# Four gate/up slabs side by side in the first FFN, and scores by pairs of heads on alternating row halves, in a two-layer encoder trunk

## The chip, the cores and the metric

The kernel runs on one core of a Trainium2 chip. The core has a matrix engine (TensorE, PE in the rows; its weight loads are PEld), VectorE (DVE), ScalarE (ACT), GpSimd (POOL) and SyncE (SP), which here issues nearly all the weight loads. The metric is the device time of one execution in microseconds, as the median of several runs.

## The reference, cut to what matters

Two layers, each with three sub-layers on 256 tokens of width 1024: a SwiGLU FFN of width 2816, a mixer with two attention branches, and a second FFN. Each is preceded by an RMS norm that is modulated with a scale and a shift taken from the conditioning `c`, and is added with a gate taken from it too.

```python
mod = c_act @ ada_w[l] + ada_b[l]
sh1, sc1, g1, sh2, sc2, g2, sh3, sc3, g3 = jnp.split(mod, N_ADA, axis=-1)
n1 = modulate(rms_norm(h, norm_g[l, 0]), sh1, sc1)
h = h + 0.5 * g1[:, None, :] * swiglu(n1, ffn_wg[l, 0], ffn_wu[l, 0], ffn_wd[l, 0])
...
# diff_attention, the second branch: two softmax maps m, four heads h, head width 64
sc = jnp.einsum('bqmhd,bsmhd->bmhqs', qi, k) * scale
p = jax.nn.softmax(sc + bias[None, None], axis=-1)      # bias = -slope * |q - k|
w = (p[:, 0] - lam * p[:, 1])
```

Inputs, weights and output are float32.

## The kernel before, in words

**Precision.** Every weight half (128 x 1024) is split into a part `whi`, rounded to the matrix engine's format, and the remainder `wlo`: ScalarE casts `whi` (line 302), VectorE subtracts (line 303). Activations are split likewise into `nh` and `nl`. A product is then three matmuls, hi-hi, lo-hi, hi-lo (`mm3`, lines 85 to 87).

**Loads.** `stream` is a list, written out by hand, of units of 128 x 2048 float32 (1 MB) in the order in which they are used. `load_next` issues the next one on SP's queue into a ring of four buffers `raw` (the first twenty units as two DMAs of half a unit). `pump(n)` takes the next n halves of the stream: a weight half is split into two of 23 slots, a `col` half becomes a column sum with `cb` on VectorE (line 235), from which the modulation's scale `ma` and shift `msh` come, and a `gate` half is added up to the residual's gate. A buffer's release lets SP issue the next load. `queue` orders such an instruction behind the one noted in `behind` for its engine.

**The order of the work.** The program's order on each engine follows from the order in which the code emits it, shifted where the planner of the tile framework sees an operand that is not ready. The code lists it by hand, in the mixer above all.

**The beginning (lines 1183 to 1203 and `first`, line 1133).** The two token halves are squared (half 0 on ScalarE, half 1 on VectorE), GpSimd makes `rstd`, VectorE scales (`xs`, line 360), TensorE transposes and ScalarE copies to `xsT`. A slab is 256 gate and 256 up columns, with the contraction of 1024 in eight chunks k; a column step `C` makes the scale and shift of two chunks, and `mod_k` turns these into `nh` and `nl`. The string `START` (line 39) has the order: `C` a pair of column units, `a` the unit with the first four chunks of the next slab, `b` the one with its last four. `go` multiplies a slab with two chunks as soon as both are there (24 matmuls). The first four slabs are done so, in four pairs of banks; then follow the down products of the finished slabs and the other seven slabs.

**The second branch's scores (`b_scores`, line 855).** For each of four heads, and each token half t: a matmul of 512 columns puts the distance bias into a bank (`idn`, a scaled identity, times `dist`), and for both maps m three matmuls of 64 rows add q.k. The heads' 64 rows are the lower or the upper half of the array by hd % 2. Then VectorE takes the maxima and ScalarE the exponentials. `b_norm` combines the two maps, `b_T` transposes them, `b_out` multiplies with v. The mixer's list (lines 1006 to 1047) puts these between the gate products `gate_mm(j, half)`, 24 matmuls each. The first branch's `a_scores` (line 788) takes two heads that lie in different row halves in turn, into two banks. All these banks are of one kind, `gen`, of which there are four.

Of the kernel before, what the change touches and what calls it, by code (L numbers as in the profile page):

```python
# [13 lines left out]
F32 = mybir.dt.float32  # L14
F32R = mybir.dt.float32r
# [4 lines left out]
P = 128  # L20
# [18 lines left out]
START = "CaCaCaabCbbb"  # L39


def trunk(tc, a):
    nc = tc.nc
    with (
# [158 lines left out]
        def load_next():  # L203
            if nload[0] < len(stream):
                u = stream[nload[0]]
                nload[0] += 1
                raw = wp.tile([P, 2048], F32, tag="raw", bufs=RAW_BUFS, name=nm("raw"))
                src = SRC[u[0]](u)
# [82 lines left out]
        def pump(n=1):  # L291
            while n > 0 and pos[0] < len(stream):
# [6 lines left out]
                if isw:  # L299
# [4 lines left out]
                    halves[u + (i,)] = (hi, lo)  # L304
# [25 lines left out]
        class Norm:  # L330
# [11 lines left out]
            def square_dve(self, hf):  # L342
                junk = b2("sq")
                x = h[self.t][:, hf * 512:(hf + 1) * 512]
                nc.vector.tensor_tensor_reduce(junk, x, x, 1.0 / 1024.0, 0.0, op0=ALU.mult, op1=ALU.add,
                                               accum_out=self.ssq[:, hf:hf + 1])
# [9 lines left out]
            def scale(self):  # L356
                self.xs = []
                for hf in range(2):
                    xs = b2("xs")
                    self.dve = nc.vector.tensor_scalar(xs, h[self.t][:, hf * 512:(hf + 1) * 512], self.rstd[:, 0:1], None,  # L360
# [166 lines left out]
        def ffn(i, nT, norm1, first, nT_next):  # L527
# [25 lines left out]
            if first is not None:  # L553
                first(hT, down)
                start = START.count("a")
                for idx in range(start == 4, start - 1):
                    down(idx)
# [115 lines left out]
        def mixer(i, nT, norm1, consts, nT_next):  # L673
# [177 lines left out]

            xs = {}
            wTs = {}

            def b_scores(hd):
                slope = 2.0 ** (-8.0 * (hd + 1) / 4.0)
                pr = slice((hd % 2) * 64, (hd % 2 + 1) * 64)
                idn = sb.tile([P, P], F32R, tag="idn", bufs=2, name=nm("idn"))
                nc.scalar.mul(idn, ident, -8.0 * slope)
                for t in range(2):  # L860
                    tok = slice(t * P, (t + 1) * P)
# [430 lines left out]
```

## Time and profile before

| | us |
|---|---|
| median of 3 runs (lowest, highest) | 1130.22 (1130.12, 1131.29) |
| the profiled execution | 1128.88 |
| its span, first to last instruction | 1127.1 |
| TensorE busy in it | 1104.9 |
| VectorE busy | 867.4 |
| ScalarE busy | 588.4 |

Busy times of the engines overlap. A busy TensorE is not one at its peak: matmuls are pipelined, so a row's duration (0.28 us for 256 columns) is longer than the distance from one start to the next, and the distance is what counts for the sum. The page has the chip's HBM read at 239 GB/s over the whole span.

### The profile page before, as it was taken

Reading aid. Unit: us, or ns where it says so; the run is one execution under the profiler, and the core shown is the slowest. Engines: PE = TensorE matmul, PEld = TensorE weight load, DVE = VectorE, ACT = ScalarE, POOL = GpSimd, SP = SyncE. Lnnn points to the kernel's source line nnn. Section 1 sums busy time; section 2 is a strip of 40 time slices with the busy share of each in tenths; the row PEclk is TensorE's granted clock in tenths of the full one; section 3 lists DMA queues with packets and bytes.
Section 4 is the critical chain, followed back from the end, with each engine's and each line's share of the span. In section 5 each row is a group of like instructions: output and inputs, shape, how many; then the busy total and the mean of one; then the engine's idle time right before and its main releaser. Section 6 shows DMA issues by size and latency. Waiting matters only on the chain.

```text
span 1127.1 us, 19136 instructions
## 1 busy us (share of the span) xinstructions
PE 1104.9 (98%) x7774; PEld 1019.7 (90%) x7774; DVE 867.4 (77%) x1334; ACT 588.4 (52%) x911; POOL 43.8 (4%) x52
## 2 busy tenths in 40 slices
PE   5999999999999999999999999999999999999997
PEld 3999999898899899999989999989889998999996
DVE  6996985899877798896489886469986778865543
ACT  4553474558664563435355544435766447544432
POOL 1000000130000000000000000004000100000000
PEclk9999999999999999999999999999999999999999
DMA  9997985368645389988439977543755454876500
GB/s 336 370 376 284 377 337 185 113 252 321 217 184 185 113 321 355 355 334 315 150 130 352 368 289 274 193 158 144 276 216 182 146 197 151 311 269 224 196 27 38
DMA packets 42584, 271.11 MB, mean 241 GB/s; under 512 B 5624, under 2 KB 6392, under 8 KB 12544
## 3 DMA queue, kind: packets, MB, share of 16 engines
q1 hardware_dynamic: 40036, 267.93, 64.2%
q10 hardware_dynamic: 2460, 1.96, 0.6%
q8 instruction: 61, 1.00, 0.3%
q14 instruction: 27, 0.22, 0.1%
HBM read 268.82 MB, written 1.05 MB: 239 GB/s over the span
## 4 chain that ended last, share of the span: by engine, by line
PE 91%; DVE 6%; issue 1%; DMA 1%; ACT 1%; POOL 1%; POOLq 0%; DVEq 0%
PE dn L87 7%; PE dn L86 7%; PE dn L85 7%; PE g L87 7%; PE u L85 7%; PE g L85 7%; PE u L87 7%; PE g L86 7%; PE u L86 7%; PE gt L85 3%; PE gt L86 3%; PE gt L87 3%; DVE wlo L303 1%; PE yb L87 1%; PE yb L86 1%; PE yb L85 1%
## 5 line engine op out<-in xcount | busy, mean ns | idle before, releaser
L303 DVE TENSOR_TENSOR wlo<-raw,whi 128x1024 fp32r<-128x1024 f32 x364 | 437.9, 1222 | 145.8 <-PE u L86 88.5
L302 ACT CAST whi<-raw 128x1024 fp32r<-128x1024 f32 x364 | 374.3, 1051 | 223.4 <-PE u L87 83.7
L85 PE MATMUL g<-nh,whi 128*128 128x256 f32 x656 | 185.0, 282 | 3.7 <-ACT nh L1145 3.7
L87 PE MATMUL g<-nl,whi 128*128 128x256 f32 x656 | 184.8, 282 | 1.6 <-DVE nl L1148 1.6
L85 PE MATMUL u<-nh,whi 128*128 128x256 f32 x656 | 184.6, 281 | 0.0
L86 PE MATMUL u<-nh,wlo 128*128 128x256 f32 x656 | 184.6, 281 | 0.0
L86 PE MATMUL g<-nh,wlo 128*128 128x256 f32 x656 | 184.4, 281 | 0.0
L87 PE MATMUL u<-nl,whi 128*128 128x256 f32 x656 | 184.3, 281 | 0.0
L85 PE MATMUL dn<-whi,hh 128*128 128x512 f32 (+1 forms) x358 | 138.5, 387 | 0.0
L87 PE MATMUL dn<-wlo,hh 128*128 128x512 f32 (+1 forms) x358 | 138.2, 386 | 0.0
L86 PE MATMUL dn<-whi,hl 128*128 128x512 f32 (+1 forms) x358 | 138.2, 386 | 0.0
L85 PEld LDWEIGHTS g<-nh,whi 128*128 128x128 f32 x656 | 123.8, 189 | 5.5 <-ACT nh L1145 4.1
L87 PEld LDWEIGHTS g<-nl,whi 128*128 128x128 f32 x656 | 125.7, 192 | 1.9 <-DVE nl L1148 1.9
L87 PEld LDWEIGHTS u<-nl,whi 128*128 128x128 f32 x656 | 126.0, 192 | 0.1
L86 PEld LDWEIGHTS g<-nh,wlo 128*128 128x128 f32 x656 | 124.2, 189 | 1.3
L86 PEld LDWEIGHTS u<-nh,wlo 128*128 128x128 f32 x656 | 124.1, 189 | 0.0
L85 PEld LDWEIGHTS u<-nh,whi 128*128 128x128 f32 x656 | 123.9, 189 | 0.0
L235 DVE CUSTOM_DVE_ANT_0 raw<-raw,cb 128x1024 f32<-128x1024 f32 x96 | 114.8, 1220 | 8.9 <-DMA raw<-in_ada_t_dram 8.9
L87 PEld LDWEIGHTS dn<-wlo,hh 128*128 128x128 f32 x358 | 67.3, 188 | 13.6
L85 PEld LDWEIGHTS dn<-whi,hh 128*128 128x128 f32 x358 | 67.3, 188 | 12.3
L86 PEld LDWEIGHTS dn<-whi,hl 128*128 128x128 f32 x358 | 67.3, 188 | 12.2
L508 ACT ACTIVATE sg<-g 128x512 f32<-128x512 f32 x41 | 24.5, 598 | 97.7 <-PE g L87 97.5
(202 smaller groups left out, 1888.5 us busy)
## 6 DMA issues: line engine op xcount, KB each, us to landing
raw<-in_w_gu_dram SPq DMA_DIRECT2D x79, 1024.0 KB, 5.9
raw<-in_w_d_dram SPq DMA_DIRECT2D x41, 1024.0 KB, 5.9
raw<-in_ada_t_dram SPq DMA_DIRECT2D x40, 1024.0 KB, 5.4
raw<-in_ada_g_dram SPq DMA_DIRECT2D x24, 1024.0 KB, 6.4
raw<-in_w_in_dram SPq DMA_DIRECT2D x16, 1024.0 KB, 4.8
raw<-in_w_gate_dram SPq DMA_DIRECT2D x16, 1024.0 KB, 4.9
raw<-in_w_gu_dram SPq DMA_DIRECT2D x18, 512.0 KB, 6.0
raw<-in_ada_t_dram SPq DMA_DIRECT2D x16, 512.0 KB, 6.1
```

The source lines that it names most:

```text
L85: nc.tensor.matmul(out, Lh, Rh, start=start, stop=False, skip_group_check=True)
L86: nc.tensor.matmul(out, Ll, Rh, start=False, stop=False, skip_group_check=True)
L87: nc.tensor.matmul(out, Lh, Rl, start=False, stop=stop, skip_group_check=True)
L235: queue("dve", nc.vector.tensor_tensor_reduce(r, r, cb, 1.0, 0.0, op0=ALU.mult, op1=ALU.add, accum_out=col[:, k:k + 1]))
L302: queue("act", nc.scalar.copy(hi, r))
L303: queue("dve", nc.vector.tensor_tensor(lo, r, hi.bitcast(F32), op=ALU.subtract))
L508: nc.scalar.activation(sg, g, AF.Silu)
```

## The change

The string `START` goes; `SIDE = 4` takes its place. At the beginning the stream is now four times: two column units, then two `side` units, each of which holds the same two K chunks of two slabs. `go` runs a step's 24 matmuls as eight hi-hi, eight lo-hi and eight hi-lo, and every step covers all four slabs. In `mod_k` the remainder `nl` is noted in `behind`, as is the second square of token half 1; the scaling `xs` at the beginning moves to ScalarE.

In the mixer `b_scores(hd)` becomes `b_scores(pair, t)`: two bias matmuls into two banks, then the twelve products of 64 rows, one head's and the other's in turn. The four `idn` are made once and kept. `b_norm` follows the pairs, and the hand-written list is rearranged.

```diff
-START = "CaCaCaabCbbb"
+SIDE = 4
@@ the stream
-                g = {x: [("gu", 0, 0, i, k) for i in range(START.count(x))] for k, x in enumerate("ab")}
-                w = [u for u in w if u not in g["a"] + g["b"]]
-                for x in START:
-                    if x == "C":
-                        stream += [c.pop(0), c.pop(0)]
-                    else:
-                        stream.append(g[x].pop(0))
+                w = [u for u in w if not (u[0] == "gu" and u[3] < SIDE)]
+                for j in range(4):
+                    stream += [c.pop(0), c.pop(0)]
+                    stream += [("side", j, p) for p in range(SIDE // 2)]
@@ load_next
+                if u[0] == "side":
+                    _, j, pr = u
+                    for i in range(2):
+                        x = slice((j % 2) * 1024, (j % 2 + 1) * 1024)
+                        nc.sync.dma_start(raw[:, i * 1024:(i + 1) * 1024], a["w_gu"][0, 0, 2 * pr + i, j // 2][:, x])
@@ Norm
-                nc.vector.tensor_tensor_reduce(junk, x, x, 1.0 / 1024.0, 0.0, op0=ALU.mult, op1=ALU.add,
+                self.dve = nc.vector.tensor_tensor_reduce(junk, x, x, 1.0 / 1024.0, 0.0, op0=ALU.mult, op1=ALU.add,
...
+                    if on_act:
+                        nc.scalar.activation(xs, h[self.t][:, hf * 512:(hf + 1) * 512], AF.Identity, scale=self.rstd[:, 0:1])
@@ the second branch
+            idns = mc.setdefault("idn", [])
+            for hd in range(len(idns), 4):
+                idns.append(const(f"idn{hd}", [P, P], F32R))
+                nc.scalar.mul(idns[hd], ident, -8.0 * 2.0 ** (-8.0 * (hd + 1) / 4.0))
...
+            def b_scores(pair, t):
+                tok = slice(t * P, (t + 1) * P)
+                scs = []
+                for hd in (2 * pair, 2 * pair + 1):
                     sc = gen("scb")
-                    nc.tensor.matmul(sc.rearrange("p (m k) -> p m k", m=2), idn, dist[:, t:t + 1, :].broadcast_to([P, 2, S]),
+                    nc.tensor.matmul(sc.rearrange("p (m k) -> p m k", m=2), idns[hd], dist[:, t:t + 1, :].broadcast_to([P, 2, S]),
                                      start=True, stop=False, skip_group_check=True)
-                    for m in range(2):
-                        ch = m * 2 + hd // 2
-                        score_mm(sc[:, m * 256:(m + 1) * 256], (st["qdT"], (pr, ch, tok)), (st["kdT"], (pr, ch, slice(0, S))), False)
+                    scs.append(sc)
+                for m in range(2):
+                    ch = m * 2 + pair
+                    for x, y in ((0, 0), (1, 0), (0, 1)):
+                        for e in range(2):
+                            pr = slice(e * 64, (e + 1) * 64)
+                            nc.tensor.matmul(scs[e][:, m * 256:(m + 1) * 256], st["qdT"][x][pr, ch, tok], st["kdT"][y][pr, ch, :],
+                                             start=False, stop=y == 1, skip_group_check=True)
@@ the mixer's list
-            b_scores(0)
+            b_scores(0, 0)
             gate_mm(1, 0)
             a_T(1, 0)
             gate_mm(1, 1)
             a_T(1, 1)
-            b_norm(0)
-            b_scores(1)
+            b_norm(0, 0)
+            b_scores(0, 1)
             gate_mm(2, 0)
             a_pv(1)
+            gate_mm(2, 1)
+            b_norm(0, 1)
+            b_scores(1, 0)
+            gate_mm(3, 0)
             b_T(0)
-            gate_mm(2, 1)
-            b_norm(1)
-            b_scores(2)
-            gate_mm(3, 0)
             gate_mm(3, 1)
             b_T(1)
-            b_norm(2)
-            b_scores(3)
+            b_norm(1, 0)
+            b_scores(1, 1)
             free(4)
             cap_w[0] = CAP2
             gate_mm(4, 0)
             gate_mm(4, 1)
+            b_norm(1, 1)
+            gate_mm(5, 0)
             b_T(2)
-            b_norm(3)
-            gate_mm(5, 0)
+            gate_mm(5, 1)
             b_T(3)
-            gate_mm(5, 1)
             b_out(0)
@@ first
             def mod_k(u):
                 pump(4)
+                pump(1)
...
-                nc.vector.tensor_tensor(nl[:, kk, :], nf, nh[:, kk, :].bitcast(F32), op=ALU.subtract)
+                behind["dve"] = nc.vector.tensor_tensor(nl[:, kk, :], nf, nh[:, kk, :].bitcast(F32), op=ALU.subtract)
...
+                for x, y in ((0, 0), (1, 0), (0, 1)):
+                    W, N = (wh, wl)[x], (nh, nl)[y]
+                    for k in (2 * u, 2 * u + 1):
+                        for c in range(2):
+                            for j, bank in ((0, g), (1, ub)):
...
+            for u in range(4):
+                mod_k(u)
+                if u % 2 == 1:
+                    free(1)
+                for sl in range(SIDE):
+                    go(sl, u)
+                    pump(1)
+                    if u == 3:
+                        if sl == 3:
+                            down(0)
+                        hT[sl] = gate_up_act(*banks[sl])
+                        pump(1)
@@ the beginning
                 if t == 1:
                     n.square_dve(hf)
+                    behind["dve"] = n.dve
...
-            n.scale()
+            n.scale(True)
```

## Rows read from the trace of the kernel before

**Rows 1.** The page: engines' busy us and share; casts' busy us, mean ns, idle before.
```profile
PE 1104.9 (98%) x7774; PEld 1019.7 (90%) x7774; DVE 867.4 (77%) x1334; ACT 588.4 (52%) x911; POOL 43.8 (4%) x52
...
L302 ACT CAST whi<-raw 128x1024 fp32r<-128x1024 f32 x364 | 374.3, 1051 | 223.4 <-PE u L87 83.7
```
**Rows 2.** TensorE's waits, 28 to 1110 us: us in total, times, longest.
```profile
PE nt L369 <- DVE xs L360: 1.0, 1, 1.0
PE pt L831 <- ACT p L820: 0.2, 1, 0.2
```
**Rows 3.** Timeline of the start: start us, us, engine, line, [idle before <-releaser].
```profile
8.55 1.23 DVE L235 CUSTOM_DVE_ANT_0 raw<-raw,cb 128x1024 f32<-128x1024 f32 x1 [8.55 <-DMA raw<-in_ada_t_dram]
9.70 0.69 DVE L345 CUSTOM_DVE_ANT_0 sq<-h 128x512 f32<-128x512 f32 x1
...
18.52 0.15 DVE L240 TENSOR_TENSOR msh<-mraw,abc 128x2 f32<-128x2 f32 x1
...
18.78 1.09 ACT L1145 ACTIVATE nh<-xsT,msh,ma 128x256 fp32r<-128x256 f32 x2 [1.22 <-DVE msh L240]
...
19.43 0.58 PE L85 MATMUL g<-nh,whi 128*128 128x256 f32 x1 [3.65 <-ACT nh L1145]
...
22.26 0.58 PE L87 MATMUL g<-nl,whi 128*128 128x256 f32 x1 [1.61 <-DVE nl L1148]
```
**Rows 4.** The chain that ended last, around 28 us: start us, us, what.
```profile
27.77 0.21 PE u L86
27.98 0.12 PE u L87
```
**Rows 5.** Stretches: us, busy (count) by engine, PEclk, DMA share, GB/s.
```profile
8.00:14.00 6.00, 1.89 (x9) 1.90 (x10) 4.57 (x13) 0.61 (x2) 1.58 (x2) 1.00 1.02 414
...
28.00:48.00 20.00, 20.00 (x178) 20.00 (x178) 19.82 (x37) 8.26 (x11) 0.00 (x0) 1.00 0.99 366
...
92.00:96.00 4.00, 4.00 (x35) 3.96 (x35) 0.00 (x0) 0.44 (x1) 0.00 (x0) 1.00 0.87 367
278.10:290.80 12.70, 12.70 (x96) 11.20 (x95) 12.57 (x33) 10.75 (x27) 0.00 (x0) 1.00 0.75 288
```
**Rows 6.** The chain that ended last, the first down product.
```profile
68.23 0.23 PE dn L85
```
**Rows 7.** Timeline of VectorE, 36 to 42 us.
```profile
36.35 0.74 DVE L1146 TENSOR_SCALAR nf<-xsT,ma,msh 128x256 f32<-128x256 f32 x2
...
38.13 0.70 DVE L1148 TENSOR_TENSOR nl<-nf,nh 128x512 fp32r<-128x512 f32 x1
...
38.74 3.50 DVE L303 TENSOR_TENSOR wlo<-raw,whi 128x1024 fp32r<-128x1024 f32 x3
```
**Rows 8.** Timeline of TensorE: twelve first-branch products, then one block of the second branch.
```profile
271.81 0.97 PE L796 MATMUL sc<-kaT,qaT 64*128 64x256 f32 x12
272.71 0.38 PE L85 MATMUL gt<-nh,whi 128*128 128x256 f32 x1
...
278.26 0.40 PE L864 MATMUL scb<-dist,idn 128*128 128x512 f32 x1
278.58 0.39 PE L85 MATMUL scb<-kd,qd 64*128 64x256 f32 x1
...
279.49 0.49 PE L864 MATMUL scb<-dist,idn 128*128 128x512 f32 x1
...
280.81 0.38 PE L85 MATMUL gt<-nh,whi 128*128 128x256 f32 x1
```
**Rows 9.** Instructions on tile scb: duration ns min/median/max, first and last start.
```profile
L877 ACT ACTIVATE xb<-scb,bi x32: 462/474/487, 281.6 to 863.0; 128x256 f32<-128x256 f32 x32
...
L871 DVE TENSOR_REDUCE nmx<-scb x16: 682/688/692, 279.6 to 860.5; 128x2 f32<-128x512 f32 x16
```
**Rows 10.** Timeline of ScalarE behind a gate product of the mixer.
```profile
316.75 0.84 ACT L957 ACTIVATE gt<-gt,bg 128x256 f32<-128x256 f32 x2 [1.38 <-PE gt L87]
317.47 0.58 ACT L898 COPY wT<-wt 128x512 f32<-128x512 f32 x1
```

More of the change, by code (lines that the diff above doesn't have):

```diff
@@ L303, in pump @@
                     queue("dve", nc.vector.tensor_tensor(lo, r, hi.bitcast(F32), op=ALU.subtract))
-                    halves[u + (i,)] = (hi, lo)
+                    if u[0] == "side":
+                        _, j, pr = u
+                        halves[("gu", 0, 0, 2 * pr + i, j // 2, j % 2)] = (hi, lo)
+                    else:
+                        halves[u + (i,)] = (hi, lo)
                 elif u[0] == "col":
@@ L354, in stats, with scale @@
                 pow_half(self.rstd, ms)
-            def scale(self):
+            def scale(self, on_act=False):
                 self.xs = []
@@ L554, in ffn @@
                 first(hT, down)
-                start = START.count("a")
-                for idx in range(start == 4, start - 1):
+                start = SIDE
+                for idx in range(1, start - 1):
                     down(idx)
@@ L877, in b_scores, with b_norm @@
                         nc.scalar.activation(x[:, y], sc[:, y], AF.Exp, bias=bi[:, m:m + 1], scale=0.125, accum_out=sm[:, m:m + 1])
-                    xs[hd, t] = (x, sm)
-            def b_norm(hd):
-                for t in range(2):
+                    xs[2 * pair + e, t] = (x, sm)
+            def b_norm(pair, t):
+                for hd in (2 * pair, 2 * pair + 1):
                     x, sm = xs[hd, t]
@@ L1135, in first @@
             banks = [[accb("g0"), accb("u0")] for _ in range(2)]
-            banks += [[gen("g0"), gen("u0")] for _ in range(START.count("a") - 2)]
+            banks += [[gen("g0"), gen("u0")] for _ in range(SIDE - 2)]
             def mod_k(u):
                 pump(4)
+                pump(1)
                 m = mods[(0, 0)]
@@ L1160, in go @@
-                done(un, i, 0)
-            seen = {"C": 0, "a": 0, "b": 0}
-            ready = [0] * len(banks)
-            for x in START:
-                if x == "C":
-                    mod_k(seen["C"])
-                    if seen["C"] % 2 == 1:
-                        free(1)
-                else:
-                    pump(2)
-                seen[x] += 1
-                for sl in range(len(banks)):
-                    n = 2 * (seen["a"] > sl) + 2 * (seen["b"] > sl)
-                    while ready[sl] < min(n, seen["C"]):
-                        go(sl, ready[sl])
-                        ready[sl] += 1
-                        if ready[sl] == 4:
-                            if sl == 3:
-                                down(0)
-                            hT[sl] = gate_up_act(*banks[sl])
-                            pump(2)
+                un, i = ("gu", 0, 0, sl, u // 2), u % 2
@@ new lines, in go @@
+                wh, wl = half(un, i)
+                for x, y in ((0, 0), (1, 0), (0, 1)):
[3 more added lines that the diff above has]
+                            for j, bank in ((0, g), (1, ub)):
+                                w = slice((k % 2) * 512 + j * 256 + c * P, (k % 2) * 512 + j * 256 + (c + 1) * P)
+                                nc.tensor.matmul(bank[:, c * 256:(c + 1) * 256], W[:, w], N[:, k, :],
+                                                 start=x + y + k + c == 0, stop=y == 1 and k == NK - 1,
+                                                 skip_group_check=True)
```

22 lines of the change are left out of this document (6 added, 16 removed).

## The prediction

> **What bounds the kernel now.** I read the busy shares first: TensorE is busy 98% of the span, VectorE 77%, ScalarE 52% [rows 1]. A busy share alone proves little, so the waits of TensorE come next: from 28 us to the end nothing but two waits, 1.2 us together, is on its list [rows 2]. So over some 1080 us every microsecond taken out of TensorE's own queue comes off the end, as long as no other engine becomes late, and time off other engines is worth nothing by itself. The exception is the start. There the timeline shows TensorE waiting: its first gate/up product is at 19.43 us, after 3.65 us for `nh`, and it stands still again until 22.26 us for `nl` [rows 3]. Then it runs until 27.9 us at 0.21 us a product [rows 4], against 20.00/178 = 0.112 us in the stretch from 28 us [rows 5], that is, at the lower of its two clocks (1.2, not 2.4 GHz). The clock column says 1.00 there too; I go by the pace of the products. In the same stretch VectorE is busy 19.82 of 20.00 us and the DMA engines 0.99, so the first slabs have three full resources, and a gain on one may be stopped by another. The chain of waits shows the stage's end, the first down product, at 68.23 us [rows 6].
>
> The profiled execution took 1128.88 us (span 1127.1 and 1.8 around it), 1.3 under the median of 1130.22. The sum is made on 1128.88 and 1.3 is put back.
>
> **Part 1, the start.** Bytes, products and the stream's order behind the first sixteen units stay as they are. What moves: (a) VectorE squares token half 1 before any column sum; (b) the four scalings `xs` go to ScalarE; (c) each of the four groups loads two column units, then the matching quarter of all four slabs, so that two K chunks feed 96 products instead of 24; (d) inside such a step the products run hi-hi, lo-hi, hi-lo, eight each, so `nl` is needed only at the seventeenth; (e) later column sums and `wlo` stand behind the group's `nl`.
>
> When does TensorE begin? The first half of the column units is in by 8.55 us, when VectorE starts on it [rows 3]. At 414 GB/s [rows 5] a half of 0.52 MB takes 1.27 us, so the fourth is there at 12.4 (8.55 + 3 x 1.27). One sum takes 1.15 us (8.55 to 9.70 [rows 3]), and VectorE can do it as halves land: the sums end at 13.5 and the shift is ready at 13.7, against 18.6 now [rows 3], because today two squares (0.69 each) and the four scalings, with their gaps, lie between the first and the second sum, and the first `wlo` ahead of the shift. Meanwhile ScalarE has the four scalings; a 128x512 copy takes it 0.58 [rows 10], so 2.3 us on an engine that has nothing to do from 8 to 13 us (0.61 busy of 6.00 [rows 5]). They cost nothing there unless they push `nh`: four scalings, sixteen transposes and four copies behind the `rstd` chain end near 13.7 as well. The first slab piece lands at about 13.7; its `whi` is 1.05 us [rows 1] and the first `nh` 0.55 (half of 1.09 [rows 3]), both on ScalarE: 15.3. I take **15.5 us** for the first product, with 14.5 (both overlap with other waiting) and 17.5 (copies and casts queue behind each other) as bounds.
>
> From there the products follow without a gap if VectorE keeps up. One group costs it four sums (4.6), four `wlo` (4 x 1.14 = 4.6), two `nf` (0.74 together), `nl` (0.70) and little else: 10.6 us [rows 3, 7]. TensorE needs 96 x 0.113 = 10.9 us for the group. That is a close race, but TensorE starts with a debt: VectorE finishes group 0 at about 20.4 us (sums to 13.5, `nf`, the first `wlo` behind its `whi` to 16, `nl`, three more `wlo`), group 1's `nh` is there near 25.7, and TensorE is through group 0 only near 28. So it has some 2.5 us of cover, kept from group to group. The wait that (e) adds holds three `wlo` behind `nl`, and behind them the raw buffers and so SP's loads; a few tenths a group, against four buffers in flight, 4 x 2.5 us of transfer. By TensorE the stage ends at 15.5 + 384 x 0.113 (43.4) + what the lower clock costs. Today the low pace lasts until 27.9 us, 5.6 us behind the last gap; at 0.21 for 0.113 that costs 2.6 us. With as much again the end is 61.5. By VectorE the last group ends at 20.4 + 3 x 10.6 = 52.2, with a few tenths per group for `nh` 53.5, and the last `nl` is wanted by TensorE at 52: the end is between 61.5 and 63. I take 62.2: **6.0 us** earlier than 68.23. Bounds: 3 us (first product at 17.5, and each group a late `nl`) and 8 us (14.5 and an earlier rise of the clock). After the stage the gain stays: between 92 and 96 us VectorE stood idle and ScalarE nearly so [rows 5], so there the producers were ahead and waited for TensorE.
>
> **Part 2, the scores of the second branch.** A block today is one head: two 512-column bias products with `idn`, each followed by six 64-row products. The timeline of TensorE shows it: 278.26 to 280.81, 2.55 us [rows 8]; the first bias product takes 0.32 with the change to 64 rows, six products 0.91. There are eight blocks (four heads, two layers). The new block has two bias products in a row and then twelve products, in turn on rows 0 to 63 and 64 to 127, into two banks. The kernel already has this pattern: the first branch's scores. Twelve such products from 271.81 to 272.71 take 0.90 us, both changes of rows included [rows 8]. The new block is then 0.23 (a 512-column product between full ones, as a down product [rows 6]) + 0.32 + 0.90 = 1.45 us, 1.10 less; eight of them give **8.8 us**. Bound below: the pairs do not overlap, and only the change to the row half and back that each block saves is won. A product alone is 0.12 (0.91 for six, 0.2 of it taken as the change back), so 0.23 + 0.32 + 12 x 0.12 + 0.2 = 2.2, and eight times 0.35 is 2.8 us. A loss is excluded by the same row: if every step from one row half to the other cost a change, twelve products could not take 0.90. Bound above: 9.5, if the bias product in front costs no change of its own. I take 8.8, since the row has the same shape and type on both operands; that the new products add to what the bias product left in the bank is the only difference.
>
> The multiplications for `idn` go from eight to four on ScalarE, which has room; nothing on the path. The weights are ready far ahead here, TensorE having no wait at all in the stretch [rows 2].
>
> What is moved can stall. A pair's two banks now fill together, so two reductions (0.69 each) and four exponentials (0.47 each [rows 9]) start at once: some 3.3 us until the banks are free. The next user of those banks is behind two half-gates, 24 products or 2.7 us each: 5.5 us of cover. `b_T(3)` now stands right ahead of `b_out(0)`, with no gate between. Behind the gate's end ScalarE has two tanh (0.84 together) and only then the copy of `wT` (0.58 [rows 10]), so the last head's operand is ready 1.4 us after the gate, while transposes and the three heads ahead of it fill about 1.1. That is a new wait of 0.3 us a layer, **0.6 us** in all, with 0 and 3 us (a 1.05 us cast ahead of the tanh in both layers) as bounds. TensorE's gates behind it wait, nothing else.
>
> **Sum.** 6.0 + 8.8 - 0.6 = 14.2; 1128.88 - 14.2 = 1114.7; with the 1.3 put back **1116.0 us**, 1.3% less.
>
> **Rivals.**
> *The pairs don't overlap* (the change does not do what it says): the bank is opened by a full-array product, which the first branch's scores don't have. Against it: row groups and banks are the same as in [rows 8]. Scores give 2.8: 1130.2 - 6.0 - 2.8 + 0.6 = 1122.0.
> *VectorE becomes the bound of the start.* For it: 19.82 of 20.00 busy [rows 5] and 10.6 against 10.9 us a group. If each group loses the 2.5 us of cover and 1 us more, the start gives 2 us instead of 6: 1120.
> *Emptying the banks sets the pace.* Two banks need 2 x 0.69 on VectorE and 4 x 0.47 on ScalarE, 3.3 us of engine time, against 1.45 of TensorE. If nothing covered that, the blocks would be no faster: 1130.2 - 6.0 = 1124. Against it: the gates between the blocks. The Trainium skill, page TensorEngine Tiling (Array Packing), section PSUM Bottleneck, has this as its rule: tiling speeds up TensorE and not the emptying of PSUM, which may then be the bound. By that rule the time would be 1124; no row of this case bears it out, TensorE not having waited for a bank in the blocks as they are.
> *Slower.* VectorE was busy 12.57 of 12.70 us around the first block [rows 5]. If its queue puts two casts and two column sums (4.6 us) ahead of a pair's reductions and norm (3.3 + some 2.5), the chain is 10.4 us against 5.5 of gates, and TensorE stands at the next block or transposes. From 14.2/8 = 1.8 us a block this eats the whole gain; at 2.5 us a block the time is 1130.2 - 14.2 + 20 = 1136.
>
> **How the numbers follow.** My forecast 0.74 (1112.5 to 1119.5 by its own bounds), no overlap 0.08, VectorE at the start 0.10, emptying 0.03, slower or a wash 0.05. Range 1112 to 1122.5: it takes in the forecast's bounds, VectorE at the start and most of no overlap, and leaves out about 0.13. About 0.2%, 2.3 us, is what a measurement can tell from no change. Faster 0.95, within 0.2% 0.02, slower 0.03.
>
> **What would show it.** Right: first gate/up product near 15.5 us, no wait of TensorE for `nl`, first down product near 62; a block of twelve score products with two bias products in 1.45 us; TensorE's list of waits still nearly empty behind 28 us. Wrong: waits for `nh` or `nl` at each group, score products 0.12 us apart, or waits for `scb`, `wT` or `xb` in the mixers. The low pace lasting 2 us longer than 5.6 would cost 1 us.

## The result, and the profile after

| us | before | after |
|---|---|---|
| median (lowest to highest, 4 runs each on the same chip) | 1130.38 (1130.12 to 1131.29) | 1117.65 (1117.24 to 1119.35) |
| the profiled execution | 1128.88 | 1117.3 |
| its span | 1127.1 | 1115.5 |

The ratio is 0.9894, with an interval of 0.9881 to 0.9907: 1.1% faster, 1.65 us short of the forecast of 1116.0 and inside the range. Against the profile's own time the sum said 14.2 us, and the two spans differ by 11.6. Where they come from is read by comparing the same product's start in both traces: the first gate/up product 3.05 us earlier, the first down product 4.4, layer 0's first mixer gate 4.7, its last mixer product 7.8, layer 1's first gate 7.6, its last mixer product 11.5, the end 11.6. So the start with the FFN behind it gave 4.7 and the two mixers 3.1 and 3.9; what the stretches between them add or lose is 0.3 us at most.

The page of after, engines' busy us and share, and TensorE's waits from 28 to 1110 us (us in total, times, longest), beside [rows 1, 2]:

```profile
PE 1097.5 (98%) x7774; PEld 1013.2 (91%) x7774; DVE 865.4 (78%) x1330; ACT 587.7 (53%) x911; POOL 44.3 (4%) x52
```
```profile
PE nt L382 <- DVE xs L373: 1.0, 1, 1.0
PE g L1184 <- ACT nh L1168: 0.4, 1, 0.4
PE pt L844 <- ACT xb L898: 0.3, 1, 0.3
PE pt L844 <- ACT p L833: 0.2, 1, 0.2
```

TensorE stays the bound; two small waits are new, one for `nh` in the start and one for `xb` in a mixer. From start to start the first is a pause of 0.6 us; the second costs 1.2 us with what follows from it, as shown below.

**The start of after**, its timeline (start us, us, engine, line, [idle before <-releaser]), beside [rows 3]:

```profile
9.94 2.00 ACT L370 ACTIVATE xs<-h,rstd 128x512 f32<-128x512 f32 x3 [1.90 <-POOL rstd L123]
...
13.20 0.72 ACT L370 ACTIVATE xs<-h,rstd 128x512 f32<-128x512 f32 x1
...
13.32 0.16 DVE L245 TENSOR_TENSOR msh<-mraw,abc 128x2 f32<-128x2 f32 x1
...
14.29 1.05 ACT L307 CAST whi<-raw 128x1024 fp32r<-128x1024 f32 x1
...
15.24 0.59 ACT L1223 COPY xsT<-nt 128x512 f32<-128x512 f32 x1
...
15.71 1.10 ACT L1168 ACTIVATE nh<-xsT,msh,ma 128x256 fp32r<-128x256 f32 x2
16.38 0.58 PE L1184 MATMUL g<-nh,whi 128*128 128x256 f32 x1 [1.29 <-ACT nh L1168]
```

The shift `msh` is there at 13.3 us against 18.5 before, as forecast (13.7). But now ScalarE is late: the scalings, the copies and a cast keep it until 15.7. The second group is where TensorE stops; VectorE's and ScalarE's timelines of after around it:

```profile
18.45 1.23 DVE L240 CUSTOM_DVE_ANT_0 raw<-raw,cb 128x1024 f32<-128x1024 f32 x1 [0.73 <-DMA raw<-in_ada_t_dram]
...
19.60 3.49 DVE L308 TENSOR_TENSOR wlo<-raw,whi 128x1024 fp32r<-128x1024 f32 x3
...
26.59 1.22 DVE L308 TENSOR_TENSOR wlo<-raw,whi 128x1024 fp32r<-128x1024 f32 x1
27.73 0.15 DVE L245 TENSOR_TENSOR msh<-mraw,abc 128x2 f32<-128x2 f32 x1
```
```profile
28.08 1.05 ACT L307 CAST whi<-raw 128x1024 fp32r<-128x1024 f32 x1 [1.00 <-DMA raw<-in_w_gu_dram]
29.04 1.09 ACT L1168 ACTIVATE nh<-xsT,msh,ma 128x256 fp32r<-128x256 f32 x2
```

VectorE is through the first group's casts at 23.0 us, not at 20.4: the first column sum of the second group (1.15 us) stood ahead of the last three, and it had waited 0.73 us for its transfer. Then come the three other sums and another `wlo`, and the second group's shift is ready at 27.9. ScalarE has meanwhile begun to wait for a slab's transfer, with the cast ahead of `nh` in its queue. TensorE begins the group at 29.68 us.

**The scores of after**, TensorE's timeline, layer 0's first two blocks, beside [rows 8]:

```profile
273.58 0.62 PE L879 MATMUL scb<-dist,idn 128*128 128x512 f32 x2
274.13 0.97 PE L887 MATMUL scb<-kd,qd 64*128 64x256 f32 x12
275.04 0.38 PE L85 MATMUL gt<-nh,whi 128*128 128x256 f32 x1
...
281.60 0.60 PE L844 MATMUL pt<-ident,p 128*128 128x128 f32 x4
282.46 0.66 PE L844 MATMUL pt<-ident,p 128*128 128x128 f32 x4 [0.26 <-ACT xb L898]
282.94 0.50 PE L879 MATMUL scb<-dist,idn 128*128 128x512 f32 x1
283.37 0.50 PE L887 MATMUL scb<-kd,qd 64*128 64x256 f32 x2
283.80 0.50 PE L879 MATMUL scb<-dist,idn 128*128 128x512 f32 x1
284.23 0.97 PE L887 MATMUL scb<-kd,qd 64*128 64x256 f32 x10
285.13 0.39 PE L85 MATMUL gt<-nh,whi 128*128 128x256 f32 x1
```

The first block takes 1.46 us (273.58 to 275.04) against 2.55 before: the forecast of 1.45. Six others take 1.45 to 1.55. The second of layer 0 takes 2.19 (282.94 to 285.13), cut in two behind a transposition `pt` that had to wait. VectorE's timeline shows for what:

```profile
276.38 0.68 DVE L892 TENSOR_REDUCE nmx<-scb 128x2 f32<-128x512 f32 x1
277.10 1.23 DVE L308 TENSOR_TENSOR wlo<-raw,whi 128x1024 fp32r<-128x1024 f32 x1
278.24 0.16 DVE L894 TENSOR_SCALAR bi<-nmx 128x2 f32<-128x2 f32 x1
278.31 1.22 DVE L308 TENSOR_TENSOR wlo<-raw,whi 128x1024 fp32r<-128x1024 f32 x1
279.45 0.68 DVE L892 TENSOR_REDUCE nmx<-scb 128x2 f32<-128x512 f32 x1
...
281.19 0.16 DVE L894 TENSOR_SCALAR bi<-nmx 128x2 f32<-128x2 f32 x1
```

ScalarE's timeline has the second bank's exponentials behind that `bi`:

```profile
281.39 0.47 ACT L898 ACTIVATE xb<-scb,bi 128x256 f32<-128x256 f32 x1 [1.33 <-DVE bi L894]
```

The first block ended at 275.0; its second reduction ran at 279.45, behind two `wlo`, its scaling `bi` only at 281.19, behind a column sum too, and ScalarE's last exponential ended at 282.3. So the pair's banks were free 7.3 us behind the block, with 6.6 us of other products (275.04 to 281.60) to cover it.

From start to start, summed by tile: the eight blocks take 12.65 us against 20.76, 8.11 less. In layer 0 `pt` takes 0.55 us more. In layer 1 the 384 gate products take 45.83 against 45.33.

### The profile page after: what moved, and what is told of

The parts are those of the page before. It is cut to its first block, busy times and chain, and to the rows that moved or that the text cites. A ratio compares the mean times of both kernels' runs of the same rounds, so it can differ in the third digit from the quotient of the medians.

```text
span 1115.5 us, 19105 instructions
## 1 busy us (share of the span) xinstructions
PE 1097.5 (98%) x7774; PEld 1013.2 (91%) x7774; DVE 865.4 (78%) x1330; ACT 587.7 (53%) x911; POOL 44.3 (4%) x52
## 4 chain that ended last, share of the span: by engine, by line
PE 88%; DVE 7%; DMA 2%; ACT 1%; issue 1%; POOL 0%; SPq 0%; POOLq 0%; DVEq 0%; ACTq 0%
PE dn L87 7%; PE dn L86 7%; PE dn L85 7%; PE u L85 6%; PE g L85 6%; PE u L87 6%; PE g L87 6%; PE g L86 6%; PE u L86 6%; PE gt L85 2%; PE gt L87 2%; PE gt L86 2%; DVE wlo L308 2%; PE g L1184 2%; PE u L1184 2%; PE yb L87 1%
## 5 line engine op out<-in xcount | busy, mean ns | idle before, releaser
L85 PE MATMUL g<-nh,whi 128*128 128x256 f32 x592 | 166.2, 281 | 0.0
L85 PE MATMUL u<-nh,whi 128*128 128x256 f32 x592 | 166.1, 281 | 0.0
L87 PE MATMUL u<-nl,whi 128*128 128x256 f32 x592 | 165.9, 280 | 0.0
L86 PE MATMUL g<-nh,wlo 128*128 128x256 f32 x592 | 165.9, 280 | 0.0
L87 PE MATMUL g<-nl,whi 128*128 128x256 f32 x592 | 165.9, 280 | 0.0
L86 PE MATMUL u<-nh,wlo 128*128 128x256 f32 x592 | 165.9, 280 | 0.0
L87 PEld LDWEIGHTS u<-nl,whi 128*128 128x128 f32 x592 | 113.0, 191 | 0.1
L86 PEld LDWEIGHTS g<-nh,wlo 128*128 128x128 f32 x592 | 111.3, 188 | 1.3
L86 PEld LDWEIGHTS u<-nh,wlo 128*128 128x128 f32 x592 | 111.3, 188 | 0.0
L85 PEld LDWEIGHTS u<-nh,whi 128*128 128x128 f32 x592 | 111.1, 188 | 0.1
```

Of the source, the lines that this page charges most:

```text
L85: nc.tensor.matmul(out, Lh, Rh, start=start, stop=False, skip_group_check=True)
L86: nc.tensor.matmul(out, Ll, Rh, start=False, stop=False, skip_group_check=True)
L87: nc.tensor.matmul(out, Lh, Rl, start=False, stop=stop, skip_group_check=True)
```

## Experiments

Each is compared with the runs of the kernel before on the same chip; the ratio's interval is in brackets. "The changed kernel" is after. Of the edits the lines that matter are shown; "..." marks a cut.

**The two parts alone.** For `start_only` the mixer of the kernel before is put into the changed kernel, for `scores_only` the other way round.

```diff
@@ start_only against the changed kernel
-            def b_scores(pair, t):
+            def b_scores(hd):
@@ scores_only against the changed kernel
-SIDE = 4
+START = "CaCaCaabCbbb"
```

> The beginning as changed, the second branch as before. Theory (two separate gains that add up): the first down product near 63.7 us as in the changed kernel, eight blocks of 2.55 to 2.64 us as before, 1130.4 - 4.4 = 1126.0 us. Rival (the start's gain is given back further on, where the producers are not far enough ahead): first down product near 63.7, but 1128 to 1130 us.

> The second branch as changed, the beginning as before. Theory (two separate gains): 3.1 us in the first mixer and 3.9 in the second, 1130.4 - 7.0 = 1123.4 us; the pause of 1.2 us around the second block of the first mixer is there too, since it comes from VectorE's queue in the mixer. Rival (that pause comes from TensorE being early after the new start): no pause, 1122.2 us.

Measured: start alone 1123.7 (0.9949 [0.9934, 0.9963]), scores alone 1123.12 (0.9944 [0.9929, 0.9959]), beside 1129.33 before: 5.6 and 6.2 us. In the traces the first stage ends 5.5 us earlier with the start alone, and this is kept to the end (6.05). The theory's 1126.0 was 2.3 us off: it took the start's gain from a single trace, and the start scatters (last experiment). The scores alone give 3.1 us in layer 0 and 3.9 in layer 1, as in after. So layer 0's stall has nothing to do with the start having moved TensorE forward. The parts are independent; each is worth what it shows alone, up to the scatter of the start (below).

**Taking the second group's pause away.** In `cast_behind` casts that are issued after a group's `nh` stay behind it on ScalarE.

```diff
-                    nc.scalar.activation(nh[:, k, :], src, AF.Identity, bias=m["sh"][:, k:k + 1], scale=m["a"][:, k:k + 1])
+                    behind["act"] = nc.scalar.activation(nh[:, k, :], src, AF.Identity, bias=m["sh"][:, k:k + 1], scale=m["a"][:, k:k + 1])
```

> The changed kernel, with ScalarE's casts that are emitted behind a step's nh held behind it in ScalarE's queue, so that no cast that waits for a DMA stands ahead of nh. Theory (the pause of TensorE at 29 us, 0.6 us long, also sets the slower pace of 0.118 us a product that lasts to the end of the stage): no pause, 0.113 throughout, first down product at 63.7 - 0.6 - 1.4 = 61.7 us, 1115.7 us. Rival (the slower pace comes from what the stage does from 29 us on, the pause is by itself): first down product near 63.1, pace 0.118 after the first group, 1117.0 us.

Measured: 1117.97 (0.9897 [0.988, 0.9913]), no gain. The pause was gone, yet the stage ended at 63.98 us. The stretch from 38 to 62 us of `start_only` and then of `cast_behind` (us, busy (count) by engine, PEclk, DMA share, GB/s) shows where it went:

```profile
38.00:62.00 24.00, 24.00 (x214) 24.00 (x213) 23.03 (x33) 15.97 (x21) 0.00 (x0) 1.00 0.99 364
```
```profile
38.00:62.00 24.00, 24.00 (x206) 24.00 (x206) 22.60 (x35) 14.02 (x19) 0.00 (x0) 1.00 0.98 370
```

The same products, TensorE never idle, the granted clock full in both: 214 products in one and 206 in the other, that is 113.3 or 117.8 ns by the products' starts (the counts take in products at the edges). I had taken the pause for the cause of the slower spacing; here it came without one. Nor does a trace without the pause show what the moved cast does: three of the six traces of the unchanged start have no pause either (`start_only`, `no_turns` and `max_first` in the table below). Over the 288 products of the last three groups the slower spacing is worth 1.3 us.

**Trying to choose the spacing.** `reset` puts one transposition, whose result is not used, ahead of each slab.

```diff
             nh, nl = nT
+            nc.tensor.transpose(g[:, 0:P], ident, ident)
             for k in range(NK):
                 un, i = unit(k)
```

> The changed kernel, with one unused 128x128 transposition ahead of each of the 37 gate/up slabs that follow down products (its result is overwritten). Theory (the pace of a run of 256-column products, 0.113 or 0.118 us, is set by how the run begins, and a transposition ahead of it gives the quicker one, as it does ahead of the gates): 96 x 0.0045 = 0.43 us less a slab, at a cost of about 0.12, so 0.3 x 32 slabs that run at 0.118 now = 9.6 us less, 1108 us. Rival (the pace comes from what the other engines do at the time, or from the banks): all slabs stay at 0.118, and the transpositions cost 37 x 0.12 = 4.4 us, 1122 us.

Measured: 1120.77 (0.9922 [0.9905, 0.9939]), 3 us slower than after. Of the 22 rows of products of a single slab three fell into 113.3 ns (11.0 us with the transposition) and 19 into 117.8 (11.42); without the transposition a slab takes 11.31 at the slower spacing. That is near the rival's 1122; the theory's 1108 is out. In the four rows of two slabs the transposition stands between the two as well, and there the second slab ran at 113.3 ns three times. In the traces of the other kernels a row of gate/up products that follows a down product ran at 117.8 ns each time, 25 times in each, and one that follows a `gb` product at 113.3 in more than half of the cases. It keeps its spacing as long as nothing comes between. What decides isn't settled.

**Turns or not.** `no_turns` runs a block's twelve products head by head.

```diff
-                for m in range(2):
-                    ch = m * 2 + pair
-                    for x, y in ((0, 0), (1, 0), (0, 1)):
-                        for e in range(2):
-                            pr = slice(e * 64, (e + 1) * 64)
+                for e in range(2):
+                    pr = slice(e * 64, (e + 1) * 64)
+                    for m in range(2):
+                        ch = m * 2 + pair
+                        for x, y in ((0, 0), (1, 0), (0, 1)):
```

> The changed kernel with one order undone: in the second branch's blocks the two bias products stay side by side, but the twelve score products run head by head (six on rows 0 to 63, then six on rows 64 to 127), not in turn. Theory (the gain of the scores comes from two products running at once on the two halves of the rows): a block of fourteen products goes from 1.45 us to about 2.2, as the block of the changed kernel in layer 0 that is cut in two by a stall hints for single products of 0.11 to 0.12; eight blocks, less the one that stalls anyway, cost 5 to 6 us, so about 1123. Rival (the gain comes from fewer changes between full rows and half rows, which this keeps): blocks stay near 1.5 us and the time near 1117.7.

Measured: 1120.45 (0.9916 [0.9901, 0.9931]), 2.8 us slower than after; neither the theory nor the rival. TensorE's timeline of one block:

```profile
273.58 0.62 PE L879 MATMUL scb<-dist,idn 128*128 128x512 f32 x2
274.13 1.32 PE L887 MATMUL scb<-kd,qd 64*128 64x256 f32 x12
275.38 0.39 PE L85 MATMUL gt<-nh,whi 128*128 128x256 f32 x1
```

A block takes 1.80 or 1.90 us, not 2.2: 0.35 more than with turns, and 0.75 less than before. So two thirds of the 1.10 us that a block gains come from having both heads' products stand together, and one third from the turns. The first two thirds have two parts. One is the saved changes between full and half rows: by the starts of the products in both traces, a block of before spends 0.33, 0.21, 0.42 and 0.20 us at its four changes, a block of after 0.23 and 0.32 us on its two bias products and 0.20 at its end, which is 0.41 us less. The other is overlap: even head by head three of the products of this block start 5 to 7 ns behind another, and three overlaps at some 0.115 us are the other 0.35. The starts fit two rows of six, one for each half, the second beginning while three of the first are still to come. The trace doesn't name the half, but it marks the products that raise a semaphore: besides the block's last one this is, in all eight blocks, the eighth or ninth of the twelve to start and not the sixth, which fits a first head that ends when two or three products of the second have begun. Layer 0's stall is missing here (no wait for `xb` in the trace). The eight blocks take 14.78 us, against 12.65 in after with the stall and 12.02 without it (`max_first`, below). By the Trainium skill, page TensorEngine Tiling (Array Packing), section Key Properties, different tiles of the array can run their weight loads and products in parallel. The trace agrees, and adds that part of the overlap (three products of six) is there even where the program has one half's products behind the other's.

**Reductions ahead of casts.** `max_first` holds what is issued after a pair's reductions behind them on VectorE.

```diff
-                    nc.vector.tensor_scalar(bi, nm_, 0.125, None, op0=ALU.mult)
+                    behind["dve"] = nc.vector.tensor_scalar(bi, nm_, 0.125, None, op0=ALU.mult)
```

> The changed kernel with one line more: casts and column sums that are issued after a pair's reductions may not run ahead of the last of them on VectorE. Theory (the 1.2 us that layer 0 loses at the second block come from a reduction that waited behind two casts): the reduction runs at once, the transposition of the first branch takes 0.8 us instead of 1.3 and the block is not cut; 1116.5 us. Rival (the casts that are now behind push something else, a weight half that a gate needs, or the other reduction still comes late): 1117.7 or more.

Measured: 1116.56 (0.9881 [0.9865, 0.9898]), where the theory had 1116.5. VectorE's timeline behind the first block, then TensorE's at the place of the stall:

```profile
277.64 0.68 DVE L892 TENSOR_REDUCE nmx<-scb 128x2 f32<-128x512 f32 x1
278.36 0.17 DVE L894 TENSOR_SCALAR bi<-nmx 128x2 f32<-128x2 f32 x1
```

```profile
283.08 1.03 PE L844 MATMUL pt<-ident,p 128*128 128x128 f32 x8
283.87 0.72 PE L879 MATMUL scb<-dist,idn 128*128 128x512 f32 x2
284.52 0.97 PE L887 MATMUL scb<-kd,qd 64*128 64x256 f32 x12
285.41 0.38 PE L85 MATMUL gt<-nh,whi 128*128 128x256 f32 x1
```

The transpositions take 0.79 us and the block 1.54. The blocks of both layers now save 4.37 us each, 8.74 in all. The gates give 0.5 a layer back, here in layer 0 too: the 384 take 45.86 us, more of them at 117.8 ns. Layer 0's mixer is therefore 0.7 us shorter than in after and not 1.2. The cause of the stall is shown; that the time fell on the forecast is in part luck, since the start scatters by more than that.

**The scalings back on VectorE.** `xs_vector`:

```diff
-            n.scale(True)
+            n.scale(False)
```

> The changed kernel with the four scalings ahead of the first transposition put back on VectorE. Theory (VectorE's sums end the start's shift, and the scalings between the sums make it later by 4 x 0.38): the shift is ready near 15 us, the first gate/up product comes at 17 to 18 us and the time is near 1119. Rival (in the changed kernel ScalarE is the late one at the first product, since it has scalings, copies and the first cast in one queue up to 15.7 us; without the scalings it is 2 us earlier): the first product stays near 16.4 or comes earlier, and the time stays within 0.5 us of 1117.7.

Measured: 1120.19 (0.9915 [0.99, 0.993]). The first product came at 18.03 us, the first down product at 65.95. ScalarE is the late engine with the scalings, but without them VectorE is later still. Not all of the 2.5 us are the start's: this trace has one more wait that no other has, 1.5 us of a `gb` product for VectorE's `gl` at 149 us.

**The old order of the three passes.** `three_by_three`:

```diff
-                for x, y in ((0, 0), (1, 0), (0, 1)):
-                    W, N = (wh, wl)[x], (nh, nl)[y]
-                    for k in (2 * u, 2 * u + 1):
+                for k in (2 * u, 2 * u + 1):
...
+                            mm3(bank[:, c * 256:(c + 1) * 256], wh[:, w], wl[:, w], nh[:, k, :], nl[:, k, :],
+                                k == 0 and c == 0, k == NK - 1)
```

> The changed kernel with the 24 products of each step of the first stage in the old order: the three passes of one operand pair next to each other, so that the low part nl is wanted at the third product and not at the seventeenth. Theory (the order buys the cover for nl): TensorE stands in each of the four groups for about the time of nf and nl behind nh, 0.7 to 1.5 us in the first and less in the later ones, where VectorE is ahead: 2 us later, about 1119.7. Rival (VectorE is ahead of TensorE from the second group on and the order costs nothing but the first wait, which TensorE spends at the lower clock anyway): within 0.7 us of 1117.7.

Measured: 1117.66 (0.9893 [0.9878, 0.9908]), unchanged. TensorE's waits name `nl` with 0.4 us:

```profile
PE g L87 <- DVE nl L1171: 0.4, 2, 0.2
```

The time doesn't have the theory's 2 us. The trace has products that start 0.3 to 0.6 us behind the one ahead of them in the first, the second and the fourth group, in the second and fourth together 1.0 us more than the spacing; but its last groups ran at 113.3 ns, and the first down product came at 64.42. So the order does buy cover in the later groups, some 1 us in this trace. In the time this is smaller than the scatter of the start, so the runs don't show a gain of the new order; only this trace does.

**The scatter of the start, and the clock.** These four were measured beside each other. `again` is the changed kernel once more. `warm` adds twelve products, whose results nobody reads, in TensorE's idle time ahead of the first product. `both` joins `max_first` and `cast_behind`, and `warm_both` is all of it.

```diff
@@ warm
+        def warm(n):
+            bank = gen("warm")
+            for _ in range(n):
+                nc.tensor.matmul(bank.rearrange("p (m k) -> p m k", m=4), onesr,
+                                 onesr.rearrange("p (o k) -> p o k", o=1).broadcast_to([P, 4, P]),
+                                 start=True, stop=True, skip_group_check=True)
+
+        warm(9)
...
             n.transposes()
+            if t == 1:
+                warm(3)
```

> The changed kernel itself once more, beside the three that follow. Its start has now been traced four times from the same code (in the changed kernel and in three experiments that edit other places): first gate/up product at 16.4 to 17.1 us, first down product at 62.6 to 65.2. Theory: the scatter is in the arrival of the first slabs and in the moment of the clock's rise, so the start's gain is 4.4 on the mean and not the 6.0 predicted; here again a value in that range and 1117.7 within 0.7 us. Rival (the changed kernel's own trace was an unlucky one, the start is nearer to the predicted 62.2): 62.5 or less and 1116.5 or less.

> The changed kernel with twelve products of 128x512 more, whose results nobody reads: nine in the 4.5 us in which TensorE stands ahead of the first transposition, three between the last transposition and the first gate/up product. Theory (the low clock, until 3.7 to 6 us behind the first product, is a cost of its own, (rise less first product)/2 = 1.8 to 3 us): the first products come 0.113 apart, the stage ends 1.8 to 3 us earlier and the time is near 1115.5. Rival (the producers bind the start: the second group's operand nh was ready at 29.0 us in the changed kernel, with TensorE already waiting 0.7 us): what the clock gives comes back as a longer wait for nh, from 0.7 to 2 us or more, and the time stays within 0.7 us of 1117.7.

> The changed kernel with two waits moved: casts that are issued after the last reduction of a pair of heads stay behind it on VectorE, and on ScalarE casts issued after a group's nh stay behind that. Theory (the first mends layer 0's stall of 1.2 us, measured alone at 1116.6; the second takes away the pause of 0.7 us at the second group, measured alone without a gain because the products then ran 0.118 apart): together 1116.2, the stall gone in both layers and no pause, whatever pace the start falls into. Rival (a start at 0.118 eats it): 1117 to 1117.7.

> The two before together: twelve idle products for the clock, and the casts behind the reductions and behind nh. Theory (the producers' cast ahead of the second group's nh is what eats the clock's gain): with it moved the gain of 1.8 to 3 us stays to 1.3 at least, and the time is 1114 to 1115. Rival (nh of the second group waits for its column sums, ready at 27.8 us in the changed kernel, not for the cast): TensorE, through the first group at about 27.4, waits about 1 us there, and the time is that of the two waits alone within 0.5 us.

Measured: `again` 1117.34 (0.989 [0.9875, 0.9905]), `warm` 1118.13 (0.9895 [0.9879, 0.9912]), `both` 1115.82 (0.9873 [0.9858, 0.9888]), `warm_both` 1116.81 (0.988 [0.9866, 0.9895]).

The table has each trace's first product, the first product of the second group, the spacing behind 38 us, and the first down product. The start's code is the same in the first six:

| | first product | second group | ns apart | first down |
|---|---|---|---|---|
| after | 16.38 | 29.68 | 117.8 | 63.70 |
| `start_only` | 16.30 | 29.94 | 113.3 | 62.58 |
| `reset` | 16.94 | 30.21 | 117.8 | 64.24 |
| `no_turns` | 16.77 | 30.58 | 113.3 | 63.22 |
| `max_first` | 17.11 | 31.26 | 117.8 | 65.18 |
| `again` | 16.84 | 30.93 | 113.3 | 65.31 |
| `cast_behind` | 16.75 | 30.06 | 117.8 | 63.98 |
| `both` | 16.80 | 29.46 | 113.3 | 62.32 |
| `warm` | 17.02 | 30.96 | 113.3 | 63.73 |
| `warm_both` | 16.18 | 29.53 | 117.8 | 63.87 |

In `again` the first products ran at the high clock almost at once, most of them 113 to 119 ns apart; in `max_first` 27 of the first ones were some 213 ns apart; in `again` and `warm_both` two. The second group began between 29.5 and 31.3 us in all of them. Stretches of `again` (us, busy (count) by engine in the order PE, PEld, DVE, ACT, POOL, then PEclk, DMA share, GB/s):

```profile
16.84:19.80 2.96, 2.96 (x25) 2.96 (x26) 1.90 (x4) 2.96 (x4) 0.00 (x0) 1.00 1.03 410
28.80:30.90 2.10, 0.31 (x3) 0.11 (x1) 1.55 (x3) 1.57 (x3) 0.00 (x0) 1.00 1.03 394
32.20:35.50 3.30, 3.30 (x18) 3.30 (x17) 3.30 (x5) 0.11 (x1) 0.00 (x0) 0.50 1.00 375
36.00:39.00 3.00, 3.00 (x29) 3.00 (x28) 3.00 (x8) 1.06 (x1) 0.00 (x0) 1.00 0.98 300
```

An early clock only lengthened the pause ahead of the second group, behind `nh`, to 2.1 us from one start to the next, with TensorE busy 0.31 us of it. Behind that the granted clock was 0.50 (1.2 GHz) from 32.2 to 35.5 us: 18 products in 3.3 us, and 29 in the 3.0 us from 36 on. This second low stretch is not free: the second group takes 12.62 us in `again` and 10.88 in `start_only`, 1.7 us more, and `again` has the latest first down product of all. Its median is within the theory's 0.7 us of 1117.7 all the same. Of `warm`, in the same columns, the stretches ahead of the first product and behind it:

```profile
10.50:13.80 3.30, 1.60 (x12) 1.06 (x10) 3.28 (x9) 1.77 (x4) 1.50 (x1) 1.00 1.02 420
...
17.10:20.60 3.50, 3.50 (x16) 3.50 (x17) 2.24 (x4) 3.18 (x4) 0.00 (x0) 0.50 1.03 411
```

The idle products had the clock up too early; by the first product, behind the waits for the scalings, it was down again. Only in `warm_both` it stayed up, and there TensorE waited 1.0 us for a `wlo` and 0.8 at the second group. So the rival's mechanism holds: what an early clock gives comes back as a wait, since the producers set the second group's beginning. In the five traces in which TensorE did not wait there (`start_only`, `no_turns`, `max_first`, `cast_behind`, `both`) the first half of `nh` was ready only 0.3 to 0.8 us ahead of it, and with nothing else changed that is the most that the low clock of the first products costs in them. `warm` alone would not show this, as its clock had fallen back. `warm_both` came out 1.0 us above `both`, where its rival had 0.5; its traced run has the slower spacing, worth 1.3.

`both` has neither stall nor pause: TensorE's list from 18 to 1110 us is

```profile
PE nt L382 <- DVE xs L373: 1.0, 1, 1.0
PE pt L844 <- ACT p L833: 0.2, 1, 0.2
```

and it has the lowest median of all, 1.5 us below `again`; its slowest run (1116.27) lies under the fastest of `again` (1116.43). Its two added lines are those shown above. How much of the 1.5 us is the scatter of the start can't be said; the part in layer 0's mixer is in each trace with the reductions first (0.7 us against after, 1.1 against `again`, whose stall was longer: `xb` 0.6 us).

## Why the prediction was right, and where its terms were off

*What bounds the kernel.* Right. What TensorE's queue lost came off the end: 4.7 + 3.1 + 3.9 = 11.7 beside 11.6 measured.

*The start, 6.0 us (bounds 3 to 8).* The mechanism was right and the size too large: 4.4 at the first down product in after, and 5.5, 3.8, 4.9, 2.9 and 2.8 in the five others with the same code, 4.0 on the mean (from its start at 68.07 us before; the chain's 68.23 is the end of the product ahead of it). The forecast's sum by TensorE had the stage end at 61.5, the six traces 64.0 on the mean. Of these 2.5 us, 1.2 are the first product, 0.2 the first group and 1.1 the last three groups:
- First product 15.5 us forecast, 16.3 to 17.1 measured, 16.7 on the mean. The shift came as forecast (13.3), but a scaling took 0.72 us and not 0.58. The fourth stood behind two copies, and the first cast ahead of the last copy. That "copies and casts queue behind each other" was in the bounds; it belonged in the value.
- The second group's `nh` near 25.7 us forecast; it began between 28.5 and 30.3 in after, `both` and `again`. The working left out that VectorE waits for a transfer before the second group's sums (0.73 us) and that a `wlo` (1.14 us) is queued ahead of the shift. The cover of 2.5 us was not there in this group. (By its own terms, 15.5 + 10.9 + 2.6, TensorE would have been through the first group at 29.0 and not at 28.) This is the rival "VectorE becomes the bound of the start", in the second group and not in the others.
- That lateness and the clock's 2.6 us lie beside each other, and the forecast added only the second, so the first group came out 13.7 us long on the mean against 13.5: right nearly by luck. `again` and `warm_both` show that with the clock up TensorE waits instead.
- The spacing of 113.3 ns was taken as given. Half of the six traces have 117.8, worth 1.3 us. In `again` the clock fell a second time, 1.7 us.

*The scores, 8.8 us.* The block's price was right: 1.45 to 1.55 us. The blocks save 8.11 us in after and 8.74 where the stall is gone. The rival without overlap falls; it had a block at 2.2. Its price was wrong too: with the turns undone a block takes 1.85, since the halves overlap even then.

*What moves can stall.* The forecast had 5.5 us of cover against 3.3 of work and named the waits of `b_T(3)`. That one cost 0.02 us a layer, not 0.3: the sixteen `wt` take 1.50 us in after and 1.49 before. The stall came elsewhere, at `a_T(1, 1)`, whose bank is behind the pair's exponentials: 1.2 us, once. It is the mechanism of the *slower* rival, casts and a column sum ahead of a pair's reductions on VectorE, at one block of eight. By the Trainium skill, page TensorEngine Tiling (Array Packing), section PSUM Bottleneck, emptying the banks may become the bound of a tiled product. The trace agrees for this one block and for no other; what decided was VectorE's order and not its load, as `max_first` shows by moving it.

*Not forecast.* The gates behind a block run more often at 117.8 ns: 0.5 us in layer 1 of after, in both layers of `max_first` and `both`.

So by terms: 6.0 forecast against 4.7; 8.8 against 8.1; 0.6 of new waits against 0.55 of `pt` and 0.55 of slower gates. Together 11.7 for 14.2: every term was off the same way. That the medians lie only 1.65 us from the forecast, and not 2.6 as the profiled executions do, is luck: the sum put back 1.3 us because the profiled execution of before was that far under its median, and that of after is 0.35 under its own.

## What to carry to other kernels

When products of half the rows come in small blocks between full ones, put two heads' products behind one change of rows, and take turns between the halves; the time to expect can be read from one existing row of such products. When two banks fill at once, pin their reductions ahead of what else the engine is given next: on a VectorE that was nearly always busy, the order and not the amount of work made the stall here. And before a low clock at the beginning is added as a term, ask which operand TensorE would wait for if it were quicker; the price is only what that wait doesn't cover, and a pause that an early clock opens can be followed by a second low stretch, as in `again`.

## What the runs showed of the hardware that was not expected

- A row of the same 128x256 products runs at one of two spacings, 113.3 or 117.8 ns, at full clock and with nothing waited for, and keeps it to its end. In after some 3,300 gate/up products stand in rows at the slower one; at 4.5 ns each that is some 15 us, more than this whole change (an estimate from the two spacings; no run had them all at the quicker one). Which one it is goes with how the row is entered: behind a down product it was the slower one every time, and one transposition ahead changed that for few rows (3 of 22 in `reset`). What decides is open.
- The granted clock falls back within the start: in `again` it was 0.50 behind a stretch in which TensorE had been busy 0.31 of 2.10 us, in `warm` behind one with 1.60 of 3.30 us busy. When it first rises differs from trace to trace of the same code, and moves the end of the stage by less than 1 us here; the second low stretch in `again` cost 1.7.
- Of the same start code the first stage ended at 62.6 to 65.3 us in six traces. A difference of 1 us in the start can't be read from one trace.
